# Sums of row quarters formed one stage ahead on GpSimd and stored, left operands built product by product, and a new memory layout, in the feed-forward of a fp32 decoder layer

## The chip, the cores and the metric

The kernel runs on one core of a Trainium2 chip. The metric is the device time of one execution in microseconds (us), the median of several runs. Below, TensorE is PE, VectorE is DVE, ScalarE is ACT, GpSimd is POOL and SyncE, whose queue issues most transfers, is SP.

## The reference

One decoder layer in fp32, sequence 2048, width 1024, feed-forward width 2816. Two groups of attention heads read one normalised input; their normalised outputs go through one output projection. What matters here comes behind that:

```python
x1 = x + concat(groups) @ w_out          # out projection and residual
h  = rmsnorm(x1, g_ffn)
a  = silu(h @ w_gate) * (h @ w_up)       # 1024 -> 2816, twice
y  = rmsnorm(x1 + a @ w_down, g_final)   # 2816 -> 1024
```

## The kernel before, in words

**Precision.** Every fp32 product is three fp32r matmuls: both operands are split into a rounded part (hi) and the rest (lo), and hi·hi, lo·hi and hi·lo are added in PSUM. The split is a cast on ACT and a subtraction on DVE or POOL.

**project_out** works through four blocks t of 512 rows: `add(t, g)` projects one head group and adds the residual on DVE (L903), `norm2(t)` (L905 to L923) squares the rows on ACT, forms their reciprocal root (`rstd_of`, L116 on DVE, L118 on POOL), multiplies them by it (L915, DVE), stores x1 (L911, SP), transposes on PE into PSUM tiles `pt` (L920), copies to `hst` (L921, ACT) and stores the transposed rows into the DRAM scratch `hT` (L923, SP). The order of calls is `add(t, 0)`, `add(t, 1)`, `norm2(t - 1)`.

**ffn_in** computes gate and up for two halves t2 of 1024 rows. A half's left matrix is cut in four quarters (rows by depth), the weights of a column pair j (0 to 10) likewise, and seven products in place of eight make a pair's quad: the left operands are A11, A12, A22 and the sums S1 = A21 + A22, S2 = S1 - A11, S3 = A11 - A21, S4 = A12 - S2; the right ones are T1 to T4 and quarters of the weights. Each product is 12 matmuls of 128x512.

- `operands(t2)` (L960 to L992) makes the 14 left tiles (seven names, hi and lo, 128x4x512). For each k of four it loads two raw buffers `hraw` from `hT` (L969; 512 KB each), forms S1, S2, S3, S4 (L979, L981, L985, L990), casts (L974) and subtracts (L975) pieces of 128x512. In the first half S3 and A12's subtraction are on POOL, A22's always.
- `weights` (L1000 to L1024) loads two raw buffers `wraw_g` or `wraw_u` (L1005, SP), forms T1 (L1011), T2 (L1013), T3 (L1017), T4 (L1021) on DVE and splits all seven (cast L996, subtraction L998).
- `quads` (L1034 to L1060) runs the seven products into three PSUM banks X, Y, Z, where later products are added onto earlier ones; between them c1 is copied on ACT (L1040) and DVE reads u2 (L1043), u3 (L1047), c22 (L1049), c21 (L1055), c12 (L1059). `first_quads` (L1062 to L1087, matmul L1069) is used for the gate of j = 0 of each half: it gives each product a bank and goes by k, so that the matmuls of a k can run when its pieces are there; seven evictions on DVE.
- `fold_down(j)` (L1089 to L1102), in the first half, loads two raw buffers of w_down, sums them on DVE and stores them as `wT`.
- `gated` is silu on ACT; `upped` multiplies (L1125) and sums (L1131 to L1138) on POOL and stores the activations `actS` (L1118) by SP, the last pair's by POOL.

**ffn_out** multiplies the stored activations by w_down with seven products as well: raw `r` (14 buffers), cast L1177, subtraction L1178 into `o` (8 buffers), matmul L1225.

**What sets the order.** The Tile framework schedules the instructions of each engine from the program order and a simulated timeline. Each engine and each queue then runs in order: what stands behind a waiting instruction waits too. One pool of four raw buffers (`rw`, 512 KB each) is shared by project_out's weights, `hraw`, `wraw_g`, `wraw_u` and `draw`; a buffer is given out in turn, and its load waits until its last readers are done. Pools lie one after another in memory, and a tile waits for those that lay at its place.

## Time and profile before

| | us |
|---|---|
| runs of the kernel before | 2407.07, 2409.79, 2407.72 |
| their median | 2407.72 |
| the profiled execution | 2404.51 |
| its span, first to last instruction | 2402.7 |
| project_out's last products, norm2 | until about 1098 |
| gate and up, first half | 1099.5 to about 1540 |
| gate and up, second half | about 1540 to 1976 |
| down projection | from 1976.9 |

The mean granted clock of TensorE is 0.985. The profile is that of one execution. In its views, a row of the windows gives the busy time of each engine in a stretch; a row of the waits gives engine, tile and line that waited, what ended the wait, and the sum, count and longest; a row of a timeline gives start, duration, engine, line, operation, output<-input, shapes, and in brackets the idle time before it and what ended that.

### The profile page before, as it was taken

The page shows a single profiled execution, that of the slowest core. Times are in us where ns is not written, and L with a number is a line of the kernel's source. Part 1 is how long each engine was busy: PE and PEld are TensorE (multiplying, and loading weights), DVE is VectorE, ACT ScalarE, POOL GpSimd, SP SyncE. Part 2 cuts the span into 40 slices and gives each one's busy share as a digit, 9 for nine tenths or more (in the row PEclk, how much of TensorE's full clock was granted, in tenths as well). Part 3 has the DMA queues.
Part 4 walks back from the last instruction along what each step waited for, and adds up shares of the span by engine and source line. Part 5 has one row for each costly group of instructions (what it writes and reads, how often), then busy time and mean ns, then how long its engine had stood idle before and what let it go on. Part 6 is the DMA issues. An engine that isn't in the chain of part 4 may idle for free.

```text
span 2402.7 us, 33903 instructions
## 1 busy us (share of the span) xinstructions
PE 2300.4 (96%) x11765; PEld 1947.0 (81%) x11765; DVE 1604.5 (67%) x3151; ACT 1054.1 (44%) x2371; POOL 468.1 (19%) x418
## 2 busy tenths in 40 slices
PE   7999999997999889897999999899999999999998
PEld 7987788886999878785888888678888878888887
DVE  5335655447999977668877776786666746557555
ACT  5323355453898862336332323342332324444442
POOL 2211211111111010113232232423232330000000
PEclk9999999998999999998999999999999999999999
DMA  7666566659988687755544544333232339768651
GB/s 220 202 189 215 159 188 173 165 157 239 222 222 219 174 244 199 241 171 203 196 155 148 175 149 167 127 127 110 91 120 92 106 115 399 240 198 283 205 189 71
DMA packets 284156, 436.21 MB, mean 182 GB/s; under 512 B 24448, under 2 KB 153088, under 8 KB 278480
## 3 DMA queue, kind: packets, MB, share of 16 engines
q1 hardware_dynamic: 279968, 423.41, 57.5%
q0 software_dynamic: 3728, 10.30, 1.5%
q8 instruction: 93, 1.52, 0.3%
q14 instruction: 79, 0.65, 0.1%
q10 hardware_dynamic: 288, 0.33, 0.0%
HBM read 286.50 MB, written 147.46 MB: 181 GB/s over the span
## 4 chain that ended last, share of the span: by engine, by line
PE 51%; DVE 5%; DMA 4%; issue 1%; POOL 0%; ACT 0%; SPq 0%; DVEq 0%; POOLq 0%; ACTq 0%
PE bY L1225 7%; PE Yu L1031 7%; PE Yg L1031 6%; PE bZ L1225 5%; PE bX L1225 5%; PE Xu L1031 4%; PE Zu L1031 4%; PE Zg L1031 4%; PE Xg L1031 4%; PE acco L893 3%; DMA ob<-oB 1%; DVE wl L998 1%; DMA draw<-in_w_down_dram 1%; DVE xs L915 1%; DMA hraw<-hT 0%
## 5 line engine op out<-in xcount | busy, mean ns | idle before, releaser
L1178 DVE TENSOR_TENSOR o<-r,o 128x1024 fp32r<-128x1024 f32 x154 | 191.2, 1252 | 131.9 <-ACT o L1177 124.1
L1177 ACT CAST o<-r 128x1024 fp32r<-128x1024 f32 x154 | 162.2, 1054 | 225.0 <-DMA r<-in_w_down_dram 50.8
L996 ACT CAST wh<-T 128x512 fp32r<-128x512 f32 x176 | 107.2, 621 | 250.1 <-PE Yu L1031 80.5
L1125 POOL TENSOR_TENSOR c<-c,c 128x512 f32<-128x512 f32 x66 | 105.2, 1594 | 567.9 <-DVE c L1049 389.4
L476 DVE TENSOR_TENSOR hl<-pt,hl 128x512 fp32r<-128x512 f32 (+1 forms) x224 | 145.6, 657 | 81.9 <-ACT hl L475 81.4
L451 ACT ACTIVATE p<-t,m 128x256 f32<-128x256 f32 (+1 forms) x384 | 177.4, 480 | 18.0 <-DVE m L676 18.0
L1225 PE MATMUL bY<-o 128*128 128x512 f32 x792 | 180.5, 389 | 0.0
L1225 PEld LDWEIGHTS bY<-o 128*128 128x128 f32 x792 | 148.6, 188 | 30.9
L177 PE MATMUL acc<-hh,wh 128*128 128x512 f32 x416 | 170.0, 409 | 0.7 <-DVE vt L247 0.7
L177 PE MATMUL acc<-hh,wl 128*128 128x512 f32 x416 | 170.4, 410 | 0.0
L177 PE MATMUL acc<-hl,wh 128*128 128x512 f32 x416 | 169.9, 408 | 0.0
L893 PE MATMUL acco<-woh,oT 128*128 128x512 f32 x512 | 163.4, 397 | 3.7 <-ACT oT L864 3.4
L998 DVE TENSOR_TENSOR wl<-T,wh 128x512 fp32r<-128x512 f32 x176 | 153.2, 882 | 0.3
L494 PE MATMUL o<-hl,v 128*128 128x128 f32 (+1 forms) x816 | 141.8, 294 | 7.2 <-DVE hl L476 5.8
L475 ACT CAST hl<-pt 128x512 fp32r<-128x512 f32 (+1 forms) x224 | 125.3, 569 | 45.2 <-PE pt L470 44.9
L429 PE MATMUL s<-k,q 128*128 128x256 f32 (+1 forms) x768 | 122.1, 290 | 18.7 <-DMA k<-kB 8.8
L470 PE MATMUL pt<-ident,p 128*128 128x128 f32 x848 | 133.7, 279 | 4.8 <-DVE hl L476 2.4
L429 PEld LDWEIGHTS s<-k,q 128*128 128x128 f32 x768 | 100.6, 191 | 26.8 <-DVE nma L566 7.4
L1225 PE MATMUL bX<-o 128*128 128x512 f32 x528 | 120.6, 389 | 1.1 <-DVE o L1178 1.1
L494 PEld LDWEIGHTS o<-hl,v 128*128 128x128 f32 x816 | 111.5, 193 | 12.4 <-DVE hl L476 9.6
L1225 PE MATMUL bZ<-o 128*128 128x512 f32 x528 | 120.3, 389 | 0.0
L893 PEld LDWEIGHTS acco<-woh,oT 128*128 128x128 f32 x512 | 96.8, 189 | 25.4 <-ACT oT L864 4.1
(465 smaller groups left out, 5801.3 us busy)
## 6 DMA issues: line engine op xcount, KB each, us to landing
r<-actS SPq DMA_DIRECT2D x154, 256.0 KB
actS<-c SPq DMA_DIRECT2D x128, 256.0 KB
wraw_g<-in_w_gate_dram SPq DMA_DIRECT2D x44, 512.0 KB
wraw_u<-in_w_up_dram SPq DMA_DIRECT2D x44, 512.0 KB
r<-wT SPq DMA_DIRECT2D x88, 256.0 KB
r<-in_w_down_dram SPq DMA_DIRECT2D x66, 256.0 KB
k<-kB SPq DMA_DIRECT2D x32, 512.0 KB
draw<-in_w_down_dram SPq DMA_DIRECT2D x22, 512.0 KB
```

The lines of the kernel that those rows point to most:

```text
L177: nc.tensor.matmul(acc, a[:, k, :], mv, start=(n == 0), stop=(n == 3 * KC - 1))
L429: nc.tensor.matmul(s[:, i, :n], b["q"], b["k"][m], start=(m == 0), stop=(m == 1))
L451: nc.scalar.activation(b["pv"](p[:, i, :n]), b["tv"](b["t"]), AF.Exp, scale=-1.0, bias=nm[:, c:c + 1], accum_out=l[:, c:c + 1])
L470: nc.tensor.transpose(pt[:, sl, :], p[:, i, hfn * P:(hfn + 1) * P], ident)
L476: nc.vector.tensor_sub(lo, pt[:, a:z, :], hi.bitcast(F32))
L494: nc.tensor.matmul(out, v[:, vi, :], mov, start=(first and n == 1), stop=(last and n == 2 * len(jobs)))
L893: nc.tensor.matmul(acc, oT[kk // 2][:, kk % 2, a, i * P:(i + 1) * P], b[:, kk, :], start=(n == 0), stop=(n == 11))
L998: nc.vector.tensor_sub(lo, src, hi.bitcast(F32))
L1031: nc.tensor.matmul(bank, a[:, k], b[:, k], start=(first and m == 0), stop=(m == 11), skip_group_check=not first)
L1177: nc.scalar.copy(o[:, 0], r)
L1178: V.tensor_sub(o[:, 1], r, o[:, 0].bitcast(F32))
L1225: nc.tensor.matmul(bank[i], o[:, u, 0, i * P:(i + 1) * P], o[:, v, 1, :], start=(first and j == 0 and m == 0), stop=(j == NP - 1 and m == ...
```

## The change

A new DRAM scratch `hS` holds, for each half, the four sums S3, S1, S2, S4. `sum_rows(t2, k)` forms them for one k, in the raw buffers: two SP loads, four POOL instructions on 128x512, two stores of 512 KB through POOL's own queue. For the first half the four calls stand in project_out behind `norm2(1)`; for the second half they stand in the first half of ffn_in, behind the up quad of j = 2, 4, 6 and 8.

`operands` then only loads and splits: for each of the seven names in turn two raw buffers of two k each, 14 loads of 512 KB, 14 casts and 14 subtractions of 128x1024 (12 on DVE, A22's 2 on POOL). `first_quads` is removed; the first gate quad goes through `quads`. The pools are laid in another order with a pad, the left operands in three pools, and in ffn_out `r` has 16 buffers and `o` two pools of four, by j's parity.

```diff
+    sc.hS = pool.tile([NT // 2, 4, P, 4, 512], F32, name="hS")
...
             norm2(t - 1, xs[t - 1])
+            if t == 2:
+                for k in range(4):
+                    sum_rows(nc, rw, sc, 0, k)
         norm2(NT - 1, xs[NT - 1])
+
+
+def sum_rows(nc, rw, sc, t2, k):
+
+    G = nc.gpsimd
+    r, q = (rw.tile([P, 2, 512], F32, tag="raw", name="sraw") for _ in range(2))
+    for a, t in enumerate((r, q)):
+        nc.sync.dma_start(t, sc.hT[2 * t2 + a].rearrange("p (b k) n -> p k b n", b=2)[:, k])
+    G.tensor_add(q[:, 1], q[:, 0], q[:, 1])
+    G.tensor_sub(q[:, 0], r[:, 0], q[:, 0])
+    G.tensor_sub(r[:, 0], q[:, 1], r[:, 0])
+    G.tensor_sub(r[:, 1], r[:, 1], r[:, 0])
+    G.dma_start(sc.hS[t2, 0:2, :, k].rearrange("s p n -> p s n"), q)
+    G.dma_start(sc.hS[t2, 2:4, :, k].rearrange("s p n -> p s n"), r)
...
-        tp, ap, gp, vp, whl, up = (pool(n, b) for n, b in (
-            ("t3", 6), ("a3", 1), ("g3", 6), ("v3", 3), ("whl3", 9), ("u3", 5)))
+        whl, tp, ap0, up, ap2, gp, vp, pad, ap1 = (pool(n, b) for n, b in (
+            ("whl3", 9), ("t3", 6), ("a30", 1), ("u3", 5), ("a32", 1), ("g3", 6), ("v3", 3), ("pad3", 1), ("a31", 1)))
+        pad.tile([P, 80], F32, name="pad3")
+        home = {"A11": ap0, "S2": ap0, "S1": ap1, "S3": ap1, "A12": ap1, "A22": ap2, "S4": ap2}
...
-            e = nc.vector if t2 else nc.gpsimd
-            for k in range(4):
...
+            for n, src in (("A11", sc.hT[2 * t2, :, 0:4]), ("S2", sc.hS[t2, 2]), ("S1", sc.hS[t2, 1]), ("S3", sc.hS[t2, 0]),
+                           ("A12", sc.hT[2 * t2, :, 4:8]), ("A22", sc.hT[2 * t2 + 1, :, 4:8]), ("S4", sc.hS[t2, 3])):
+                for ks in (slice(0, 2), slice(2, 4)):
                     raw = rw.tile([P, 2, 512], F32, tag="raw", name="hraw")
+                    nc.sync.dma_start(raw, src[:, ks])
+                    hi, lo = S[n][0][:, ks], S[n][1][:, ks]
+                    nc.scalar.copy(hi, raw)
+                    (nc.gpsimd if n == "A22" else nc.vector).tensor_sub(lo, raw, hi.bitcast(F32))
...
-                if j:
-                    quads(S, views[0], j, "g", "g", gated)
-                else:
-                    first_quads(S, w0, "g", gated)
+                quads(S, views[0], j, "g", "g", gated, None if j else w0)
                 if t2 == 0:
                     fold_down(j)
                 quads(S, views[1], j, "u", "v", upped)
+                if t2 + 1 < NT // 2 and j in (2, 4, 6, 8):
+                    sum_rows(nc, rw, sc, t2 + 1, j // 2 - 1)
...
-        rp, op, xp, cp, sp = (pool(n, b) for n, b in (("r4", 14), ("op4", 8), ("x4", 3), ("c4", 1), ("s4", 2)))
+        rp, op0, xp, cp, sp, pad, op1 = (pool(n, b) for n, b in (
+            ("r4", 16), ("op40", 4), ("x4", 3), ("c4", 1), ("s4", 2), ("pad4", 1), ("op41", 4)))
+        pad.tile([P, 2900], F32, name="pad4")
```

How the instructions move is shown at three places. The lines of the changed kernel differ by a few: its loads of the sums are L956, the sums L957 to L960, their stores L961 and L962, the loads of the operands L989, their subtraction L992, the weights' load L1006, T1 to T4 L1012 to L1022, the split L999, u3 L1048, the reciprocal root L120, the store of hT L925 and that of x1 L913.

First, SP at the end of project_out, where ffn_in begins. `xs` are rows of x with the residual, `hst` transposed rows. Before (the first gate weights stand some 75 rows further up):

```order
L923 DMA hT<-hst 128x2048 x2
L838 DMA xs_11600<-in_x_dram 128x1024 x3
L969 DMA hraw<-hT 128x2x512
L911 DMA x_71<-xs_11600 128x1024 x4
L969 DMA hraw<-hT 128x2x512
L923 DMA hT<-hst 128x2048 x2
L969 DMA hraw<-hT 128x2x512
L923 DMA hT<-hst 128x2048 x2
L969 DMA hraw<-hT 128x2x512 x4
```

And now:

```order
L925 DMA hT<-hst 128x2048 x2
L840 DMA xs_11641<-in_x_dram 128x1024 x3
L956 DMA sraw<-hT 128x2x512 x7
L913 DMA x_71<-xs_11641 128x1024 x2
L1006 DMA wraw_g<-in_w_gate_dram 128x4x256
L913 DMA x_71<-xs_11641 128x1024 x2
L1006 DMA wraw_g<-in_w_gate_dram 128x4x256
L989 DMA hraw<-hT 128x1024
L925 DMA hT<-hst 128x2048 x2
L989 DMA hraw<-hT 128x1024
L989 DMA hraw<-hS 128x1024 x2
```

The loads of the sums stand ahead of the last stores of x1, and the first gate weights have moved down behind them.

Second, POOL in the same stretch; `rs_o` and `rs_f` are the reciprocal roots of the last add and of norm2. Before:

```order
L118 TENSOR_TENSOR rs_o_11825<-ms_o_11823,half 128x4
L118 TENSOR_TENSOR rs_f_0_11908<-ms_f_0_11906,half 128x1
L118 TENSOR_TENSOR rs_f_1_11928<-ms_f_1_11926,half 128x1
L118 TENSOR_TENSOR rs_f_2_11948<-ms_f_2_11946,half 128x1
L118 TENSOR_TENSOR rs_f_3_11968<-ms_f_3_11966,half 128x1
```

And now:

```order
L957 TENSOR_TENSOR sraw<-sraw 128x512
L120 TENSOR_TENSOR rs_o_11866<-ms_o_11864,half 128x4
L120 TENSOR_TENSOR rs_f_0_11949<-ms_f_0_11947,half 128x1
L958 TENSOR_TENSOR sraw<-sraw 128x512
L959 TENSOR_TENSOR sraw<-sraw 128x512
L961 DMA hS<-sraw 128x2x512
L957 TENSOR_TENSOR sraw<-sraw 128x512
L960 TENSOR_TENSOR sraw<-sraw 128x512
L120 TENSOR_TENSOR rs_f_1_11969<-ms_f_1_11967,half 128x1
L958 TENSOR_TENSOR sraw<-sraw 128x512
```

The roots now stand between the sums of the third and the fourth k and their stores.

Third, DVE in the first half around a sum (the end of j = 4), where the gate weights after next are made; `wl` are lo parts of weights, `T` the sums T1 to T4, `u` and `c` evictions. Before:

```order
L1011 TENSOR_TENSOR T_13768<-wraw_g 128x512
L1047 TENSOR_TENSOR u_13393<-Yu,c_13353 128x512
L1125 TENSOR_TENSOR gate<-Xu,gate 128x512
L998 TENSOR_TENSOR wl<-T_13482,wh 128x512
L1049 TENSOR_TENSOR c_13395<-Zu,u_13393 128x512
L998 TENSOR_TENSOR wl<-wraw_g,wh 128x512
L998 TENSOR_TENSOR wl<-wraw_u,wh 128x512
L1013 TENSOR_TENSOR T_13770<-wraw_g,T_13768 128x512
L1055 TENSOR_TENSOR c_13425<-Yu,c_13353 128x512
```

And now:

```order
L1012 TENSOR_TENSOR T_13785<-wraw_g 128x512
L1056 TENSOR_TENSOR c_13432<-Yu,c_13360 128x512
L999 TENSOR_TENSOR wl<-T_13621,wh 128x512
L1060 TENSOR_TENSOR c_13453<-Zu,u_13374 128x512
L999 TENSOR_TENSOR wl<-T_13633,wh 128x512
L999 TENSOR_TENSOR wl<-wraw_u,wh 128x512
L1014 TENSOR_TENSOR T_13787<-wraw_g,T_13785 128x512
L1018 TENSOR_TENSOR T_13797<-wraw_g 128x512
L1022 TENSOR_TENSOR T_13807<-wraw_g,T_13787 128x512
L1048 TENSOR_TENSOR u_13554<-Yg,c_13514 128x512
```

T1 and T2 have moved behind some of the up quad's evictions, and u3 of the next gate quad (`Yg`) stands right behind T2, T3 and T4.

More of the change, by code (lines that the diff above doesn't have):

```diff
@@ L960, in operands @@
         def operands(t2):
[L962 to L991 removed]
+            S = {n: [p_.tile([P, 4, 512], F32R, tag=f"{n}{u}", name=f"{n}{u}") for u in "hl"] for n, p_ in home.items()}
+            for n, src in (("A11", sc.hT[2 * t2, :, 0:4]), ("S2", sc.hS[t2, 2]), ("S1", sc.hS[t2, 1]), ("S3", sc.hS[t2, 0]),
+                           ("A12", sc.hT[2 * t2, :, 4:8]), ("A22", sc.hT[2 * t2 + 1, :, 4:8]), ("S4", sc.hS[t2, 3])):
+                for ks in (slice(0, 2), slice(2, 4)):
+                    raw = rw.tile([P, 2, 512], F32, tag="raw", name="hraw")
+                    nc.sync.dma_start(raw, src[:, ks])
+                    hi, lo = S[n][0][:, ks], S[n][1][:, ks]
+                    nc.scalar.copy(hi, raw)
+                    (nc.gpsimd if n == "A22" else nc.vector).tensor_sub(lo, raw, hi.bitcast(F32))
             return S
@@ L1032, in product, with quads @@
                     m += 1
-        def quads(S, view, j, nm, tag, done):
-            w = weights(view, j, nm)
+        def quads(S, view, j, nm, tag, done, w=None):
+            w = w or weights(view, j, nm)
             X, Y, Z = (ps.tile([P, 512], F32, tag="mm", name=f"{b}{nm}") for b in "XYZ")
@@ L1059, in quads @@
             nc.vector.tensor_add(c12, Z, u2)
-            done(0, 1, c12, False)
-        def first_quads(S, w, tag, done):
-            bank = {n: ps.tile([P, 512], F32, tag="mm", name=f"F{n}") for n in S}
-            for k in range(4):
-                for n in S:
-                    (hi, lo), (wh, wl) = S[n], w[n]
-                    for m, (a, b) in enumerate(((wh, hi), (wl, hi), (wh, lo))):
-                        nc.tensor.matmul(bank[n], a[:, k], b[:, k], start=(k == 0 and m == 0), stop=(k == 3 and m == 2))
-            c1 = tmp("u", "c1")
-            nc.scalar.copy(c1, bank["A11"])
-            u2 = tmp("u", "u2")
-            nc.vector.tensor_add(u2, bank["S2"], c1)
-            c11 = tmp(tag, "c11")
-            nc.vector.tensor_add(c11, bank["A12"], c1)
-            done(0, 0, c11, False)
-            c12 = tmp(tag, "c12")
-            nc.vector.tensor_add(c12, bank["S1"], u2)
-            u3 = tmp("u", "u3")
-            nc.vector.tensor_add(u3, bank["S3"], u2)
-            c22 = tmp(tag, "c22")
-            nc.vector.tensor_add(c22, bank["S1"], u3)
-            done(1, 1, c22, False)
-            c21 = tmp(tag, "c21")
-            nc.vector.tensor_add(c21, bank["A22"], u3)
-            done(1, 0, c21, False)
-            nc.vector.tensor_add(c12, bank["S4"], c12)
             done(0, 1, c12, False)
@@ L1175, in operands @@
                 nc.sync.dma_start(r[:, 1], wdv[:, f, hf * 512:(hf + 1) * 512])
-            o = op.tile([P, 2, 2, 512], F32R, tag="o", name="o4")
+            o = (op1 if j % 2 else op0).tile([P, 2, 2, 512], F32R, tag="o", name="o4")
             nc.scalar.copy(o[:, 0], r)
```

25 lines of the change are left out of this document (removed).

## The prediction, made blind

> **What bounds the kernel now.** I read the page's busy times first, then the windows over the two starts of the gate and up stage, then TensorE's waits there, then the tile of the loads. The page:
>
> ```profile
> span 2402.7 us, 33903 instructions
> PE 2300.4 (96%) x11765; PEld 1947.0 (81%) x11765; DVE 1604.5 (67%) x3151; ACT 1054.1 (44%) x2371; POOL 468.1 (19%) x418
> ```
>
> TensorE is busy for 96%, so time can be won only where it starves. Windows around the places that the change touches follow; the columns are the stretch, its length, busy us (x instructions) of PE, PEld, DVE, ACT and POOL, the granted clock, the DMA share and GB/s.
>
> ```profile
> 1080.00:1100.00 20.00, 14.08 (x88) 12.11 (x87) 15.57 (x23) 14.04 (x28) 4.33 (x6) 0.93 0.59 219
> 1100.00:1120.00 20.00, 15.74 (x42) 11.16 (x42) 17.48 (x18) 12.13 (x23) 13.32 (x9) 0.65 0.57 205
> 1120.00:1140.00 20.00, 16.22 (x61) 12.07 (x61) 20.00 (x27) 9.92 (x17) 5.76 (x4) 0.91 0.51 169
> 1520.00:1540.00 20.00, 20.00 (x90) 16.54 (x89) 13.62 (x20) 8.13 (x14) 3.24 (x3) 1.00 0.23 77
> 1540.00:1560.00 20.00, 13.57 (x47) 9.19 (x45) 15.83 (x18) 6.63 (x11) 11.98 (x8) 0.83 0.50 165
> 1560.00:1580.00 20.00, 17.16 (x64) 11.01 (x64) 20.00 (x30) 11.45 (x21) 2.76 (x2) 1.00 0.43 140
> 1960.00:1980.00 20.00, 18.11 (x78) 14.31 (x78) 8.96 (x10) 4.96 (x6) 9.29 (x8) 1.00 0.54 181
> ```
>
> An undisturbed stretch does 90 matmuls in 20 us, 0.222 us each. The second start (1540 to 1580) does 111 where 180 would fit: 69 x 0.222 = 15.3 us lost. The first (1100 to 1140) does 103 of 180, 17.1 us lost, behind a stretch of transposes. The start of the next stage (1960 to 1980) does 78 of 90: 2.7 us lost. TensorE's waits name who ends them, with sum, count and longest:
>
> ```profile
> PE FS L1069 <- ACT S3h L974: 5.1, 2, 3.0
> PE FS L1069 <- DVE S2l L975: 4.0, 2, 2.8
> PE pt L920 <- DVE xs L915: 15.5, 7, 4.7
> ```
>
> So both starts wait for left operands, and before the first one the transposes wait for norm2. VectorE is full behind it (20.00 of 20 us in two windows). The tile of the raw loads shows what one piece costs (min/median/max ns):
>
> ```profile
> L974 ACT CAST A11h<-hraw x8: 605/620/624, 1098.9 to 1560.0; 128x512 fp32r<-128x512 f32 x8
> L975 DVE TENSOR_TENSOR A11l<-hraw,A11h x8: 679/693/1775, 1099.5 to 1562.7; 128x512 fp32r<-128x512 f32 x8
> L975 POOL TENSOR_TENSOR A22l<-hraw,A22h x8: 1568/1722/1741, 1102.5 to 1562.9; 128x512 fp32r<-128x512 f32 x8
> ```
>
> **The change part by part.** Prices of the new forms stand in the page's groups (busy us, mean ns):
>
> ```profile
> L1178 DVE TENSOR_TENSOR o<-r,o 128x1024 fp32r<-128x1024 f32 x154 | 191.2, 1252 | 131.9 <-ACT o L1177 124.1
> L1177 ACT CAST o<-r 128x1024 fp32r<-128x1024 f32 x154 | 162.2, 1054 | 225.0 <-DMA r<-in_w_down_dram 50.8
> L1125 POOL TENSOR_TENSOR c<-c,c 128x512 f32<-128x512 f32 x66 | 105.2, 1594 | 567.9 <-DVE c L1049 389.4
> ```
>
> *Second start.* Removed from VectorE: 24 subtractions, 16 sums and 2 of 7 evictions. The two windows from 1540 hold 48 instructions in 35.83 us, 0.746 each, so the old 47 are 35.1 us. The new ones are 12 x 1.252 + 5 x 0.746 = 18.8 us. One wait on GpSimd goes as well:
>
> ```profile
> 1548.44 1.73 DVE L985 TENSOR_TENSOR s<-hraw 128x512 f32<-128x512 f32 x1 [1.16 <-POOL c L1133]
> ```
>
> The 16.3 us freed exceed the 15.3 lost. By product, the casts can also run as each product of the last up quad releases its tile, where the old order by k needed all seven tiles at once. I leave 3 us for what stays: 14 loads turn in four buffers, and two GpSimd subtractions of twice the 1.72 us above come before A22. **-12**, between -15.3 (all) and -3 (the turn of the buffers replaces VectorE as the bound).
>
> *First start.* The order changes most here: the gate weights, loaded long ahead before, stand behind four sums, all through the same four raw buffers. The rows of before:
>
> ```profile
> 1049.69 0.56 SPq L969 DMA_DIRECT2D hraw<-hT  x1
> 1071.66 1.39 POOL L118 TENSOR_TENSOR rs_o<-ms_o,half 128x4 f32<-128x4 f32 x1 [21.94 <-DVE ms_f L116]
> 1095.82 1.28 DVE L915 SCALAR_TENSOR_TENSOR xs<-xs,rs_f,gf 128x1024 f32<-128x1024 f32 x1 [0.72 <-POOL rs_f L118]
> 1099.54 0.80 PE L1069 MATMUL FA<-A11h,wh 128*128 128x512 f32 x1 [0.34 <-ACT A11h L974]
> 1134.29 0.39 PE L1031 MATMUL Xu<-A11h,wh 128*128 128x512 f32 x1
> ```
>
> A load can start at 1049.7 and, by the weight load below, lands 3.6 us later. From 1053.3 GpSimd has 16 x 1.594 = 25.5 us of sums and eight issues of 0.56 (4.5 us): not done before 1083.3, and later by the stores' landings. The reciprocal roots of the last add and of norm2 now stand between these instructions in GpSimd's queue (before they found it idle for 21.94 us). A sum there that waits for its load holds the multiply of L915, and the transposes behind it, which already wait 15.5 us for it. I put that at 3 us: loads of the operands turn from 1102, not 1099. A turn of four is 3.6 + 1.05 + 1.25 and an issue of 0.56, about 6.5 us. Three turns take it to 1121.5, the last pieces of S4 are split at 1127.4, the up weights take the buffers then and land at 1131.0; a cast and a subtraction (0.62 + 0.69) and five instructions ahead on VectorE (three sums of w_down and two evictions, 0.69 each) give 1135.8 for the first up matmul, against 1134.3: **+1.5**. The low end, -4, is no delay of norm2 and a shorter first turn. The high end, +12, is two store landings in series and the roots held by 4 us more.
>
> *The four sums inside the first half.* At the end of j = 2, 4, 6 and 8 the two loads take the place of the next gate weights on SP, and the second weight load waits till a sum's store has landed. VectorE's T2 waits for that load, and the eviction u3 stands behind T2, T3 and T4; the matmuls of A22 may not add to bank Y before u3 has read it. Rows of one such place before, and two that show VectorE's pitch of 0.60:
>
> ```profile
> 1270.63 0.37 SPq L1005 DMA_DIRECT2D wraw_g<-in_w_gate_dram  x1
> 1274.24 0.69 DVE L1013 TENSOR_TENSOR T<-wraw_g,T 128x512 f32<-128x512 f32 x1 [3.04 <-DMA wraw_g<-in_w_gate_dram]
> 1265.11 0.69 DVE L1017 TENSOR_TENSOR T<-wraw_u 128x512 f32<-128x512 f32 x1
> 1265.71 0.69 DVE L1021 TENSOR_TENSOR T<-wraw_u,T 128x512 f32<-128x512 f32 x1
> 1282.72 0.39 PE L1031 MATMUL Yg<-S3h,wh 128*128 128x512 f32 x1
> 1285.44 0.39 PE L1031 MATMUL Xu<-A11h,wh 128*128 128x512 f32 x1
> 1290.66 0.39 PE L1031 MATMUL Yg<-A22h,wh 128*128 128x512 f32 x1
> ```
>
> What GpSimd's own stores take to land (the dma view's last number, and the line of the activations' tile, in us):
>
> ```profile
> oA<-rawa POOLq DMA_DIRECT2D x64, 128.0 KB, 3.7
> actS<-c POOLq DMA_DIRECT2D x6, 256.0 KB, 5.8
> DMA to landing us min/median/max: 2.4/5.6/6.5
> L1118 POOL DMA_DIRECT2D actS<-c x6: 539/562/592, 1971.5 to 1985.3; - x6
> ```
>
> No row has 512 KB from GpSimd. I take 4 us, near the 128 KB row: the 256 KB rows fell where the next stage's loads begin. Then: 1270.6 + 3.6 (load) + 4.8 (three GpSimd instructions) + 0.6 (issue) + 4.0 + 3.6 (weights) = 1287.2, and T2, T3, T4, u3 at 0.60 each make 1289.6. In the changed order of j = 5, 7 and 9, A22 comes after the 12 matmuls of Xu and one of Yu, at 1285.44 + 2.72 + 0.23 = 1288.4. So TensorE waits 1.2 us three times and some 0.5 at the first: **+4**, from 0 (landing 2.8 us or less) to +14 (6.5 us).
>
> The Trainium skill (DMA: Bandwidth & Descriptors, Anatomy of one DMA, SWDGE path) gives a GpSimd-issued DMA 2.0 us and its bytes at 436 GB/s. By that, an estimate, 512 KB land in 3.2 us, the stalls would shrink to about 1.5 us in all, and the whole sum would be -10; the trace's 256 KB rows, with a median of 5.6 us, are over twice what the rule makes of them.
>
> *GpSimd beside VectorE.* Those 16 instructions take 25.5 us in which VectorE's own stretch: the row of A11l goes from 0.69 to 1.775 us. This stands in a stretch where VectorE has 6 us free of 20 (13.62 busy), so I cost it at nothing; without that cover it would be up to 25 us x (1 - 0.69/1.775), 15 us.
>
> The Trainium skill (SBUF — State Buffer, Who interferes with whom) says that VectorE and GpSimd share one pair of ports, and that an instruction of VectorE with two SBUF inputs is held by a GpSimd one that reads SBUF. The stretched row agrees with it; it speaks against moving work to GpSimd, but changes no term.
>
> *Start of the last stage.* The new layout and 16 raw buffers let loads start earlier:
>
> ```profile
> 1976.91 13.46 PE L1225 MATMUL bX<-o 128*128 128x512 f32 x58 [1.10 <-DVE o L1178]
> ```
>
> Of 2.7 us lost, this 1.1 can go: **-1** (0 to -2.7); the rest of the stage runs without a wait, so more buffers bring nothing there.
>
> Sum: -12 + 1.5 + 4 - 1 = -7.5. The profiled execution took 2404.5 us (span 2402.7), so 2397.0 there; it lay 3.2 below the median of the runs, 2407.7, on which the forecast stands: **2400.2**.
>
> **Rivals.**
>
> *The hops are cheap.* Stores land within 2.8 us: no stall at the sums, and the first start gains its 4: -12 - 4 - 1 = -17, 2390.7. For it: the 2.4 us minimum above; against it: that row's median of 5.6. The 3.2 us that the Trainium skill gives (same section as above) lie close to it.
>
> *The gain is given back.* With stores that land in 5 to 5.6 us, each of three sums stalls 2.4 and the first 1 (+8), and the first start is 4 late: -12 + 8 + 4 - 1 = -1, 2406.7. For it: the very median; against it: the DMA share is 0.23 to 0.57 in the windows above, not full.
>
> *Slower: the raw buffers are the bound.* Four buffers now carry operands, weights, w_down and sums, and a sum holds two of them for load, arithmetic and store. If a store takes 6.5 us, the stalls come to 14; in the first project_out, GpSimd's roots stand behind sums that wait for these same buffers, +10: -12 + 14 + 10 - 1 = +11, 2418.7. It decides as soon as stalls and first start together exceed 17.8 us. For it: L915 is already waited for, by 15.5 us; against it: the landing would have to be the slowest of those rows every time.
>
> That the change does less than it says (VectorE's work at the second start isn't what bounds it) is the -3 end of the first term: +1.5, within the third case.
>
> **How the numbers follow.** Forecast (-5 to -12): 0.38. Cheap hops: 0.18. Given back: 0.20. Slower: 0.24. A change of 0.2%, 4.8 us, is about what a measurement of this kernel can tell from none. Faster is the first two, 0.56; the same 0.20; slower 0.24. The range goes from 2389 (cheap hops with a little more) to 2419 (the slower case's own time), leaving out the best ends of all terms and the slower case's tail, some 0.17; the forecast's own range is 2395.7 to 2402.7.
>
> **What would show it.** Right: the second start at 170 or more matmuls in its 40 us, waits there of 3 us at most; VectorE behind T2 at the sums of j = 4, 6, 8 with TensorE idle 1 to 1.5 us ahead of A22; stores from GpSimd landing near 4 us; the first up matmul near 1136. Wrong: TensorE waiting for raw loads in the second start; L915 waiting for GpSimd by more than 4 us in all more than now; landings near 6 us; or a wait that is in none of these places, above all of evictions behind stretched VectorE work.

## The result and the profile after

The changed kernel took 2429.47 us (median of 4 runs, 2428.33 to 2431.27), the kernel before 2408.76 beside it: a ratio of 1.0087, 95% interval 1.007 to 1.0105. It is slower by 20.7 us, outside the forecast's range (2389 to 2419) and on the other side.

The page after:

```profile
span 2427.2 us, 33945 instructions
PE 2318.6 (96%) x11765; PEld 1956.7 (81%) x11765; DVE 1592.6 (66%) x3099; ACT 1051.7 (43%) x2343; POOL 504.4 (21%) x454
```

TensorE has the same 11765 matmuls and is busy for 18 us longer; the span grew by 24.5. The windows of the changed kernel, columns as in the prediction:

```profile
1080.00:1100.00 20.00, 14.04 (x76) 11.77 (x74) 17.84 (x25) 11.04 (x20) 18.82 (x18) 0.83 0.85 308
1100.00:1120.00 20.00, 12.05 (x46) 8.53 (x46) 13.40 (x16) 12.27 (x21) 0.56 (x1) 0.83 0.97 370
1120.00:1140.00 20.00, 15.83 (x57) 10.50 (x55) 13.04 (x13) 11.77 (x13) 4.70 (x2) 0.91 0.76 260
1220.00:1240.00 20.00, 16.97 (x67) 13.48 (x67) 16.07 (x22) 5.66 (x10) 2.41 (x3) 0.91 0.62 214
1240.00:1260.00 20.00, 18.65 (x81) 14.77 (x80) 13.85 (x18) 4.87 (x9) 5.42 (x4) 1.00 0.39 131
1560.00:1580.00 20.00, 20.00 (x89) 16.43 (x88) 15.66 (x17) 10.65 (x12) 9.03 (x5) 1.00 0.77 263
1580.00:1600.00 20.00, 17.67 (x70) 13.88 (x69) 20.00 (x25) 9.31 (x17) 8.80 (x5) 0.91 0.66 207
```

The second start (now about 1547 to 1609) lost only one stretch, 70 matmuls where 90 fit. TensorE's waits there sum to 2.3 us, 1.5 for u3 and 0.8 for an up weight; none is for a left operand any more. The middle of the first half now has holes (67 and 81), in stretches that were full before:

```profile
1220.00:1240.00 20.00, 20.00 (x90) 16.57 (x89) 14.85 (x25) 6.91 (x12) 1.62 (x1) 1.00 0.58 195
1240.00:1260.00 20.00, 20.00 (x90) 16.57 (x89) 13.81 (x18) 6.81 (x13) 9.59 (x6) 1.00 0.39 136
```

And a full stretch does 89 matmuls, not 90. Longer windows show that last point better, one in the second half of gate and up and one in the last stage, in both of which TensorE waits for nothing. Before, then after:

```profile
1760.00:1800.00 40.00, 40.00 (x178) 33.12 (x177) 27.40 (x36) 12.87 (x23) 11.40 (x7) 1.00 0.30 100
2280.00:2320.00 40.00, 40.00 (x178) 33.12 (x177) 20.16 (x19) 15.69 (x15) 0.00 (x0) 1.00 0.62 196
```

```profile
1760.00:1800.00 40.00, 40.00 (x177) 32.85 (x176) 25.50 (x35) 12.76 (x22) 12.67 (x8) 1.00 0.32 104
2280.00:2320.00 40.00, 40.00 (x176) 32.78 (x175) 20.68 (x19) 17.28 (x23) 0.00 (x0) 1.00 0.62 196
```

At the same granted clock of 1.00 and with an engine that is busy throughout, fewer matmuls fit. The traces hold each matmul's start. The mean distance between successive starts (those above 300 ns, the stalls, left out) is the pitch used below: 226.7 ns before in both places, 228.5 and 229.3 after.

With the same starts the whole difference can be cut at equal places of the work: the first matmul of the out projection, the first of gate and up, matmuls number 168, 1764 and 2016 of their 3696, their last, and the last of the down projection.

| stretch (us) | before | after | difference | forecast |
|---|---|---|---|---|
| until the out projection | 875.1 | 878.1 | +3.0 | 0 |
| out projection, norm2 | 224.4 | 226.8 | +2.4 | first start: |
| first start, matmuls to 168 | 55.6 | 58.7 | +3.1 | +1.5 for both |
| rest of the first half, to 1764 | 364.9 | 383.8 | +18.9 | +4 |
| second start, to 2016 | 72.8 | 62.0 | -10.8 | -12 |
| rest of the second half | 381.7 | 384.6 | +2.9 | 0 |
| last stage | 420.3 | 425.1 | +4.8 | -1 |
| behind it | 7.9 | 8.2 | +0.3 | 0 |

In the rest of the first half, distances above 260 ns sum to 2.7 us beyond that bound before and to 17.9 after: +15.2 is stall, the rest pitch. Not all of the stall is waiting: 3.6 of the 17.9 us are 28 matmuls started 0.26 to 0.5 us apart, a good half of them in two spells of 3.4 us, from 1228.1 and from 1262.3, for which the trace grants a clock of 0.50. These spells stand shortly behind the two longest waits (3.0 and 3.3 us below); the first shows as the 0.91 of the window at 1220. The kernel before has no such spell in this half. The first row is code that the change didn't touch; over the 17 profiles of this study it lies anywhere between 874.5 and 881.9, and it is not explained further.

TensorE's waits in the first half behind the start, before and then after:

```profile
PE Yu L1031 <- DVE u L1043: 1.0, 2, 0.6
PE Yg L1031 <- DVE u L1043: 0.9, 1, 0.9
```

```profile
PE Yg L1032 <- DVE u L1048: 6.8, 4, 3.0
PE Yg L1032 <- DVE u L1044: 4.9, 3, 3.3
PE Yu L1032 <- DVE u L1044: 1.5, 1, 1.5
```

As forecast, TensorE waits for u3 (L1048), and for u2 (L1044) too, which stand on VectorE behind T1 to T4, which wait for weights. SP's waits name what loads of weights wait for in turn, before and then after:

```profile
SPq L1005 <- DMA wT<-draw: 29.9, 16, 4.5
```

```profile
SPq L1006 <- DMA hS<-sraw: 26.9, 4, 8.9
SPq L1006 <- DMA wT<-draw: 20.1, 11, 3.1
```

Four times a load of weights waited for the store of a sum, 6.7 us on average. Before, the only stores that such loads waited for were those of `fold_down`, 29.9 us in all; now both kinds make 47.0. But VectorE's own waits for gate weights grew by little, from 24.0 to 29.3 us (before, then after):

```profile
DVE T L1013 <- DMA wraw_g<-in_w_gate_dram: 20.3, 10, 3.0
DVE T L1011 <- DMA wraw_g<-in_w_gate_dram: 3.7, 7, 0.8
```

```profile
DVE T L1014 <- DMA wraw_g<-in_w_gate_dram: 16.9, 9, 3.8
DVE T L1012 <- DMA wraw_g<-in_w_gate_dram: 12.4, 8, 3.5
```

So what stands behind such a wait in VectorE's order must count as well as how long it is. The stores themselves (tile hS, ns and then us):

```profile
L961 POOL DMA_DIRECT2D hS<-sraw x8: 733/757/769, 1060.8 to 1454.1; - x8
DMA to landing us min/median/max: 3.2/4.5/5.8
```

### The profile page after: what moved, and what is told of

The parts are those of the page before. It is cut to its first block, busy times and chain, and to the rows that moved or that the text cites. A ratio compares the mean times of both kernels' runs of the same rounds, so it can differ in the third digit from the quotient of the medians.

```text
span 2427.2 us, 33945 instructions
## 1 busy us (share of the span) xinstructions
PE 2318.6 (96%) x11765; PEld 1956.7 (81%) x11765; DVE 1592.6 (66%) x3099; ACT 1051.7 (43%) x2343; POOL 504.4 (21%) x454
## 3 DMA queue, kind: packets, MB, share of 16 engines
q1 hardware_dynamic: 284000, 438.09, 58.6%
## 4 chain that ended last, share of the span: by engine, by line
PE 61%; DMA 14%; DVE 12%; ACT 5%; issue 3%; POOL 3%; SPq 2%; DVEq 0%; POOLq 0%; ACTq 0%
PE bY L1199 7%; PE acc L179 7%; PE Yu L1032 5%; PE bZ L1199 5%; PE bX L1199 5%; PE Yg L1032 5%; PE accv L246 4%; PE s L431 3%; PE Xu L1032 3%; PE Zu L1032 3%; PE Zg L1032 3%; PE Xg L1032 3%; PE pt L472 3%; ACT p L453 2%; DVE wl L999 2%
## 5 line engine op out<-in xcount | busy, mean ns | idle before, releaser
L999 DVE TENSOR_TENSOR wl<-T,wh 128x512 fp32r<-128x512 f32 x176 | 159.7, 915 | 0.2
L496 PEld LDWEIGHTS o<-hl,v 128*128 128x128 f32 x816 | 113.4, 196 | 11.8 <-DVE hl L478 10.4
L435 DVE CUSTOM_DVE_ANT_0 t<-s,tab 128x256 f32<-128x256 f32 (+1 forms) x344 | 113.0, 369 | 9.4 <-PE s L431 6.8
```

What stands on the lines that cost most here:

```text
L496: nc.tensor.matmul(out, v[:, vi, :], mov, start=(first and n == 1), stop=(last and n == 2 * len(jobs)))
L999: nc.vector.tensor_sub(lo, src, hi.bitcast(F32))
```

## The experiments

Two theories stood at the outset. *Placement*: the pitch of a matmul depends on where its two operands lie, and the new layout put them badly. Its rival was traffic: GpSimd and DMA beside the matmuls. *Buffers*: the stalls of the first half come from four raw buffers that now also carry the sums, and from the loads behind them on SP. Its rivals were GpSimd's work beside VectorE and the store through GpSimd's queue.

Each kernel was timed beside the kernel before on the same chip, and the ratios are to that. The sets of runs were on different chips, so between sets the ratios compare better than the medians. The stretches are cut as above, and each row of them is one profiled execution; those of e5 and e10 are the fastest of their kernels' runs, those of e6 and e14 the slowest. From e5 to e14 every kernel also has the pads of e1 and is set against e1's first half (383.6 us).

| run | until out proj. | out proj. | first start | first half | second start | second half | last stage | median, ratio [95%] |
|---|---|---|---|---|---|---|---|---|
| e1_phase | 876.9 | 226.9 | 59.9 | 383.6 | 63.4 | 381.4 | 420.3 | 2424.3, 1.0080 [1.0060, 1.0101] |
| e2_before_shift | 875.3 | 223.0 | 56.1 | 372.6 | 74.0 | 392.8 | 421.1 | 2425.0, 1.0082 [1.0064, 1.0101] |
| e3_first_old | 881.3 | 221.6 | 56.8 | 386.3 | 63.9 | 384.5 | 425.1 | 2428.5, 1.0092 [1.0077, 1.0107] |
| e4_no_math | 879.4 | 226.4 | 59.8 | 390.2 | 62.3 | 384.5 | 425.1 | 2437.1, 1.0131 [1.0114, 1.0147] |
| e5_fold_later | 875.6 | 225.7 | 60.4 | 373.2 | 62.0 | 381.5 | 420.3 | 2414.3, 1.0033 [1.0018, 1.0048] |
| e6_later_first_old | 881.9 | 223.7 | 56.9 | 372.7 | 62.5 | 382.6 | 420.3 | 2404.1, 0.9990 [0.9974, 1.0006] |
| e7_sums_dve | 880.7 | 226.7 | 58.6 | 373.6 | 61.8 | 381.4 | 420.3 | 2413.4, 1.0028 [1.0016, 1.0041] |
| e8_sum_for_fold | 875.7 | 226.3 | 59.0 | 373.7 | 62.2 | 381.4 | 420.3 | 2408.5, 1.0010 [0.9996, 1.0023] |
| e9_later_dve | 876.8 | 225.7 | 60.5 | 370.6 | 64.5 | 381.5 | 420.3 | 2410.0, 1.0005 [0.9994, 1.0015] |
| e10_all | 874.7 | 221.1 | 56.7 | 383.5 | 62.1 | 383.5 | 420.3 | 2416.2, 1.0037 [1.0023, 1.0051] |
| e11_folds_second | 876.1 | 219.8 | 54.5 | 378.1 | 66.6 | 386.2 | 420.3 | 2412.2, 1.0015 [1.0004, 1.0026] |
| e12_sp_store | 876.7 | 221.7 | 56.6 | 370.2 | 62.1 | 384.8 | 420.3 | 2402.8, 0.9986 [0.9968, 1.0005] |
| e13_gpsimd_store | 878.4 | 223.3 | 56.5 | 370.6 | 62.5 | 381.9 | 420.3 | 2402.4, 0.9988 [0.9975, 1.0001] |
| e14_sp_store_folds | 877.8 | 223.4 | 57.0 | 385.1 | 64.2 | 381.7 | 420.3 | 2412.2, 1.0020 [1.0009, 1.0032] |
| e15_before_phase | 874.5 | 222.0 | 56.1 | 367.2 | 72.6 | 381.9 | 420.3 | 2403.9, 1.0001 [0.9987, 1.0014] |

### Placement

The pools' sizes give every tile's address. In the kernel before, both operands of every gate, up and down matmul start at byte 224 modulo 512. The pad of 80 floats (320 bytes) in the changed kernel puts S1, S3 and A12 at 32, and the pad of 2900 puts the operands of every odd j of the last stage at 192. The first run repairs just that.

**e1_phase**

```diff
-        pad.tile([P, 80], F32, name="pad3")
+        pad.tile([P, 128], F32, name="pad3")
...
-        pad.tile([P, 2900], F32, name="pad4")
+        pad.tile([P, 2908], F32, name="pad4")
```

> Only the two pads of the changed kernel are other sizes (80 to 128 and 2900 to 2908 elements), so that all operands of the feed-forward matmuls start at the same byte modulo 512. Theory of placement: the pitch of undisturbed matmuls falls from 229 ns to the 227 ns of the kernel before, 3,700 x 2.3 + 1,850 x 2.6 ns = 13 us less, 2416 us. Rival (the pitch is slower because of GpSimd's and the DMAs' traffic, or by chance of the run): 2429 us as now.

**e2_before_shift** does the opposite to the kernel before: the split weights lie 320 bytes further, all else in place.

```diff
-        tp, ap, gp, vp, whl, up = (pool(n, b) for n, b in (
-            ("t3", 6), ("a3", 1), ("g3", 6), ("v3", 3), ("whl3", 9), ("u3", 5)))
+        tp, ap, gp, vp, pad, whl, up = (pool(n, b) for n, b in (
+            ("t3", 6), ("a3", 1), ("g3", 6), ("v3", 3), ("pad3", 1), ("whl3", 9), ("u3", 5)))
+        pad.tile([P, 80], F32, name="pad3")
```

> The kernel before with a pad of 320 bytes ahead of the split weights in the gate and up stage, nothing else. Theory of placement: its matmuls there go from 227 to about 229 to 230 ns, 3,700 x 2.5 ns = 9 us more, 2418 us, and the last stage stays at 227 ns. Rival (traffic): no change, 2409 us.

The same two windows, of e1_phase first and then of e2_before_shift:

```profile
1760.00:1800.00 40.00, 40.00 (x178) 33.11 (x177) 25.86 (x35) 12.64 (x22) 12.65 (x8) 1.00 0.32 107
2280.00:2320.00 40.00, 40.00 (x178) 33.15 (x177) 20.68 (x19) 17.79 (x23) 0.00 (x0) 1.00 0.62 197
```

```profile
1760.00:1800.00 40.00, 40.00 (x173) 32.25 (x172) 26.11 (x34) 11.99 (x21) 11.58 (x8) 1.00 0.30 99
2280.00:2320.00 40.00, 40.00 (x178) 33.13 (x177) 20.68 (x19) 17.69 (x23) 0.00 (x0) 1.00 0.61 197
```

With one phase in the whole feed-forward the changed kernel is back at 178 in both, with all its sums and DMAs in place; the kernel before falls to 173 in the stage that was shifted (pitch 233.3 ns) and keeps 178 in the other. Placement is shown, and traffic is out. The changed kernel's own second half says the same product by product: S1, S3 and A12, the shifted ones, ran at 228.9 to 230.6 ns from start to start, A11 and A22, which follow shifted ones or stand between them on TensorE, at 229.7 and 228.2, and S2 and S4 at 226.7; in e1 all seven are at 226.7 or 226.8. The size was missed both ways: the shift cost twice what was expected (2425.0 for 2418), and the repair brought 8.0 us in the two undisturbed stretches (384.6 to 381.4 and 425.1 to 420.3), but nothing in the first half (383.6), whose stalls rose from 17.9 to 20.3 us. That VectorE and the loads, not the matmuls, set the pace there is a reading that fits, not a test. Between the two sets of runs the median fell by 5 us, not 13, and the kernel before's own by 2.4; the ratio went only from 1.0087 to 1.0080, which these runs don't tell from no change. What the repair is worth rests on the two stretches.

**e15_before_phase** asks whether the rule holds where the change never was. In the out projection of both kernels the operands differ by 320 bytes.

```diff
-        op, wp0, wp1, cp, sp, xp, hp, slot = (pool(n, b) for n, b in (
-            ("op", 2), ("wo30", 1), ("wo31", 1), ("c3", 1), ("s3", 2), ("x3", 2), ("hst", 2), ("slot", 6)))
+        op, wp0, wp1, cp, sp, xp, hp, pad, slot = (pool(n, b) for n, b in (
+            ("op", 2), ("wo30", 1), ("wo31", 1), ("c3", 1), ("s3", 2), ("x3", 2), ("hst", 2), ("pad5", 1), ("slot", 6)))
+        pad.tile([P, 80], F32, name="pad5")
```

> The kernel before with one edit: the pad of 320 bytes in the out projection. Theory of placement: the pitch of its matmuls falls from 229.2 to 227.4 ns and the out projection gets 1.5 to 2 us shorter; the whole 2 us, too little to be told from none by the times alone. Rival: no change in pitch.

The pitch fell from 229.2 to 227.6 ns and the stretch from 224.4 to 222.0 us. The whole (1.0001) can't be told from none, as expected: the first half was 2 us longer in that profile.

### The first start

**e3_first_old** leaves out the four sums in the out projection and takes `operands(0)` and the first gate quad from the kernel before.

```diff
-            if t == 2:
-                for k in range(4):
-                    sum_rows(nc, rw, sc, 0, k)
...
-                quads(S, views[0], j, "g", "g", gated, None if j else w0)
+                if t2 == 0 and j == 0:
+                    first_quads(S, w0, "g", gated)
+                else:
+                    quads(S, views[0], j, "g", "g", gated, None if j else w0)
```

> The changed kernel with the first half's operands and first gate quad as before (no sums in the out projection); the sums for the second half stay. Theory that the first start lost by its four sums standing ahead of the gate weights and of norm2: the stretch from the first out-projection matmul to the 168th gate and up matmul shortens by about 5 us, 2424 us. Rival (that stretch is only late by chance, or by the placement): at most 1 us less.

Out projection and first start together took 278.4 us, against 285.5 with the sums and 280.0 before: the sums there cost 7.1. The median moved only by 1 us, and the ratio not at all for the better (1.0092 for 1.0087), since the first half behind it was 2.5 and the second start 1.9 us longer, and the untouched part before it 3.2. A part of what the sums cost stands in GpSimd's timeline of the changed kernel:

```profile
1077.07 1.29 POOL L957 TENSOR_TENSOR sraw<-sraw 128x512 f32<-128x512 f32 x1 [6.66 <-DMA sraw<-hT]
1078.32 1.04 POOL L120 TENSOR_TENSOR rs_o<-ms_o,half 128x4 f32<-128x4 f32 x1
```

The third sum waited 6.66 us for a load that had waited for the first sum's store, and the reciprocal root behind it came 6.7 us later than before (1078.32 for 1071.66). From 1040 to 1160 TensorE's transposes waited 7.4 us, for 5.6 before, and its first products 11.6 us for operands and weights, for 8.4. SP took 24.49 us to issue the seven loads of sums in a row:

```profile
1051.47 24.49 SPq L956 DMA_DIRECT2D sraw<-hT  x7
```

### The stalls of the first half

**e4_no_math** leaves out the 16 GpSimd instructions of the sums in the first half (`if t2 == 0:` ahead of them), so that its second half works on rows that were never summed. It keeps the pads of the changed kernel.

> The changed kernel in which the four sums of the first half load and store their raw rows but leave out the four GpSimd instructions each (the second half's S operands are not sums). Theory that GpSimd's trains of instructions keep VectorE waiting: the stalls of TensorE in the first half fall from 18 us to about 6, 2418 us. Rival (the two raw buffers held until the stores have landed, and the gate weights behind them on SP): at most 4 us less, since only 5 of some 16 us of holding go.

It became slower, 390.2 us in the first half with 24.2 us of stalls. The sums' arithmetic is not the cause by itself. Their two raw buffers do hold up loads: at one of the sums SP's timeline and VectorE's wait read

```profile
1277.70 8.87 SPq L956 DMA_DIRECT2D sraw<-hT  x2
1287.78 7.44 SPq L1007 DMA_DIRECT2D wraw_g<-in_w_gate_dram  x2
```

```profile
1293.57 0.69 DVE L1013 TENSOR_TENSOR T<-wraw_g 128x512 f32<-128x512 f32 x1 [7.05 <-DMA wraw_g<-in_w_gate_dram]
```

The second load of the sum got a buffer only 8 us after the first, the gate weights came behind both, and VectorE stood 7.05 us, with evictions behind it. Why it lost more than with the arithmetic is not settled; the order of the engines is another one in that kernel.

**e5_fold_later**: `fold_down`, too, takes two raw buffers for load, sums and store, in each pair of the first half, though its results are needed only in the last stage.

```diff
-                if t2 == 0:
+                if (t2 == 0) == (j not in (2, 4, 6, 8)):
                     fold_down(j)
```

> The changed kernel with operands at one phase (the pads of the run before), and the sums of w_down (fold_down) of j = 2, 4, 6 and 8 moved into the second half, where nothing needs them before the last stage. So each sum of rows takes the two raw buffers that a sum of w_down took. Theory that the four raw buffers and the loads queued behind them on SP cause the stalls: the first half (matmul 168 to 1764) falls from 383.6 us to about 367, its stalls from 20 to 4 us, the second half stays below 384; 2408 us in all. Rival (the sum's own hops or GpSimd's work beside VectorE): the first half stays above 378 us, 2420 us.

The first half fell from 383.6 to 373.2 us, 10.4 of the 16.6 that were expected, its stalls from 20.3 to 10.4, and the second half took the four folds at no cost (381.5). The gate weights came no sooner for it: VectorE waited for them 29.6 us, for 27.9 in e1. What fell is its wait for the raw rows of `fold_down`, from 22.1 to 13.9. So a fold costs not only by its buffers. Its four sums stand in VectorE's queue too, as three rows ahead of the longest stall of the changed kernel show (others stand between them):

```profile
1253.09 0.69 DVE L1014 TENSOR_TENSOR T<-wraw_g,T 128x512 f32<-128x512 f32 x1 [3.77 <-DMA wraw_g<-in_w_gate_dram]
1254.98 1.70 DVE L1070 TENSOR_TENSOR draw<-draw 128x512 f32<-128x512 f32 x1
1261.17 0.68 DVE L1044 TENSOR_TENSOR u<-Yg,c 128x512 f32<-128x512 f32 x1
```

No run gave the sums buffers of their own with all folds in place, so buffers, loads and VectorE's share of a fold are not parted. About half of what is left in e5 is regular: stalls of 1.1 to 1.4 us ahead of A22 in the gate quads of j = 2, 4, 6 and 8. VectorE and GpSimd at one of them:

```profile
1292.19 0.87 DVE L1014 TENSOR_TENSOR T<-wraw_g,T 128x512 f32<-128x512 f32 x1 [0.83 <-DMA wraw_g<-in_w_gate_dram]
1292.99 1.77 DVE L1018 TENSOR_TENSOR T<-wraw_g 128x512 f32<-128x512 f32 x1
1294.68 1.78 DVE L1022 TENSOR_TENSOR T<-wraw_g,T 128x512 f32<-128x512 f32 x1
1296.39 0.68 DVE L1048 TENSOR_TENSOR u<-Yg,c 128x512 f32<-128x512 f32 x1
```

```profile
1292.60 1.62 POOL L1106 TENSOR_TENSOR c<-c,gate 128x512 f32<-128x512 f32 x1
1294.18 1.74 POOL L1108 TENSOR_TENSOR c<-gate,c 128x512 f32<-128x512 f32 x1
```

This is the stall that the prediction described, T2, T3, T4 and u3 behind the late weights, and nearly its size. T3 and T4 took 1.77 and 1.78 us where 0.60 was counted, while GpSimd ran beside them.

**e6_later_first_old** joins this with e3's edit.

> As the run with fold_down moved, and the first half's operands and first gate quad as in the kernel before (no sums in the out projection). Theory: another 6 us at the first start (from the out projection's first matmul to the 168th of gate and up, 279 us instead of 286), 2401 us, faster than both kernels. Rival (what is saved at the start is lost behind it, as in the run with the old first half alone): 2407 us.

Out projection and first start took 280.6 us, the first half 372.7: the saving at the start stayed this time, and the kernel was level with the kernel before (0.9990, interval 0.9974 to 1.0006), 3 us short of the expectation.

**e7_sums_dve** moves the arithmetic of the second half's sums to VectorE, with all folds in place; the stores stay on GpSimd's queue.

```diff
-    G = nc.gpsimd
+    G = nc.vector if t2 else nc.gpsimd
```

> The kernel with one phase in which the arithmetic of the four sums in the first half is on VectorE (16 instructions of 0.69 us) instead of GpSimd, all else the same. Theory of the raw buffers: a sum's buffers come free 3 us earlier, the stalls of the first half fall by 2 to 5 us of 20, 2421 us. Rival (GpSimd's instructions lock VectorE out): they fall by 10 us or more, 2414 us.

By its numbers the rival won: the first half fell by 10 us, to 373.6. Buffers come free sooner as well when four instructions take 0.69 us each, so this run alone can't tell the two.

**e8_sum_for_fold** calls the sums ahead of the up quad, where the moved folds had stood.

> As the run with fold_down moved, but the sums of rows stand in the program where fold_down stood, ahead of the up quad instead of behind it. Theory of the raw buffers and SP's order: the stalls are as small as there or smaller, since SP then has the same order as before the change with other loads in two places: first half 366 us, 2407 us. Rival (the store through GpSimd's queue, behind its work for the up quad, holds the buffers): first half above 372 us.

373.7 us for the first half, like e5: the place within the pair made no difference there (the medians, 2408.5 and 2414.3, lie further apart than these two profiles). The number asked of the theory (366) was missed, and the rival's bound (372) passed.

**e9_later_dve** joins e5 and e7.

> Both remedies of the stalls in the first half at once, with operands at one phase: fold_down of j = 2, 4, 6, 8 moved into the second half, and the sums' arithmetic in the first half on VectorE. If the two work on different parts of the stalls (buffers taken from the rotation; GpSimd's instructions), they add up: 20 us less twice 10, the first half near 366 us. If both shorten the same wait (the gate weights behind a buffer that a sum holds), the first half stays near 371 us.

370.6 us: two remedies of 10 us each make 13 together, not 20. They mostly shorten one wait.

**e10_all** (e6, e7 and the pad of the out projection) and **e11_folds_second** (the same, `fold_down` only `if t2 == 1`).

> As that, with the first half's operands as in the kernel before, and a pad of 320 bytes in the out projection that brings its operands to one phase too. Theory of placement: the pitch of the out projection's matmuls falls from 229.2 to 227 ns, 768 x 2.3 = 2 us, though the change never touched that stage. Whole: first start 6 us better than the changed kernel's, first half 366, second start 62, so some 8 us below the kernel before, 2398 us. Rival: the first half stays at 371 us as the two remedies shorten the same wait, 2403 us.

> As the last, with all eleven sums of w_down in the second half. Theory of the raw buffers: the first half has two fewer buffers to turn in every pair of columns but the four with sums, and falls below the kernel before's 364.9 us, to 363, with its stalls gone; the second half, which had 1 us of stalls, gains no more than 2 us. 2396 us. Rival: the second half, whose loads then queue behind the folds, loses 4 us or more.

Both fell short. In e10 the first half went back to 383.5 us, with stalls of 4.0 to 4.1 at the sums of j = 4, 6 and 8. On VectorE the sum now waits itself for its load, with everything behind it, and one of two subtractions further on is held by GpSimd for 4.55 us (the last section tells of that):

```profile
1271.08 0.69 DVE L955 TENSOR_TENSOR sraw<-sraw 128x512 f32<-128x512 f32 x1 [4.70 <-DMA sraw<-hT]
1277.83 6.25 DVE L1027 TENSOR_TENSOR wl<-T,wh 128x512 fp32r<-128x512 f32 x2
```

The two are not parted. The same edit that gained 10 us in e7 thus cost 13 here (383.5 for the 370.6 of e13, which differs by it alone): the gain is no property of the engine that adds; it hung on that kernel's order. In e11, with no fold left in the first half, it still took 378.1 us, with 15.1 of stalls, so buffers that the folds free do not by themselves end the stalls. The second half lost 4.5 us, as the rival said (4 or more), where the theory allowed 2. The out projection's pitch, 227.5 and 227.4 ns, came as expected.

**e12_sp_store** and its control **e13_gpsimd_store**: e6 with the pad of the out projection; in e12 SP issues the sums' stores.

```diff
-    G.dma_start(sc.hS[t2, 0:2, :, k].rearrange("s p n -> p s n"), q)
-    G.dma_start(sc.hS[t2, 2:4, :, k].rearrange("s p n -> p s n"), r)
+    nc.sync.dma_start(sc.hS[t2, 0:2, :, k].rearrange("s p n -> p s n"), q)
+    nc.sync.dma_start(sc.hS[t2, 2:4, :, k].rearrange("s p n -> p s n"), r)
```

> Operands at one phase (the out projection's too), the first half's operands as in the kernel before, four folds of w_down moved into the second half, the sums of rows on GpSimd as in the changed kernel, but their stores issued by SP. Theory that a store through GpSimd's own queue costs: the issue of 0.75 us stands in GpSimd's train and the landing is longer; the next gate weights wait for it. Then the first half falls from 373 us (the same kernel with GpSimd's stores) to 369 or less; about 2398 us. Rival (SP, in order, waits for the sum and holds the activations' stores and the gate weights behind it): first half 373 us or more.

> The same with the stores through GpSimd's queue, as in the changed kernel. It differs from the run with four folds moved and the first half as before only by the out projection's phase: out projection at 227.4 instead of 229.1 ns, 1 to 2 us less than that run's 2404 us beside 2406 of the kernel before, so faster than the kernel before by 4 us.

370.2 and 370.6 us for the first half: the queue of the store makes no difference there. Both stand 2.7 to 3 us below the kernel before by their medians (2402.8 and 2402.4 beside 2405.45), with intervals that reach 1.0005 and 1.0001: the best versions of the study, and not told from the kernel before.

**e14_sp_store_folds** puts the folds back into e12.

> As the run with the sums' stores issued by SP (first half 370.2 us), but with all sums of w_down back in the first half, as in the changed kernel. Theory of the raw buffers: with two more buffers to turn in four pairs, stalls of 15 to 20 us return, first half 378 to 384 us, 2413 us. Rival (the store through GpSimd's queue was the cause): first half stays at 370 us, 2403 us.

385.1 us, 15 more than e12, by this one edit; by the medians it is 9 more (2412.2 for 2402.8), and e14's profile is that of its slowest run. VectorE's waits for gate weights rose from 33.8 to 42.7 us, those for the raw rows of the folds from 9.9 to 20.1. Sums and folds in the same pairs carry most of the stalls, by the raw buffers and by what the folds add to SP and VectorE together; the store's queue carries none that can be seen.

## Why the prediction was wrong, point by point

**Second start.** Forecast -12, measured -10.8: right in size, and the waits for left operands are gone as forecast. The start was less full than its sign asked, 158 matmuls in the 40 us from 1547 and not 170. Which share VectorE's fewer, larger instructions have in it and which the order by product was not tried.

**The four sums in the first half: the step that failed.** It read "TensorE waits 1.2 us three times and some 0.5 at the first: +4", from 0 to +14. Measured: +15.2 of stalls. The single stall was described well (e5: 1.1 to 1.4 us four times, though in the gate quads of j = 2, 4, 6 and 8, not in those that the prediction names), and the landing of 4 us was near the 4.5 measured. The step failed in counting one delayed gate load at each sum and nothing else. In the changed kernel the pairs of j = 2, 4, 6 and 8 have 7.5 us of stalls, those of j = 1, 3, 5 and 9 another 7.1. Three things stand in its place. A sum's two raw buffers, beside the two of a fold, hold up the loads behind them, by the stalls' places those of the next pair too, and VectorE's sums of w_down stand in the same queue as what waits for these loads: taking the folds out of the sums' pairs brought 10 us (e5), putting them back cost 15 (e14 against e12; 9 by the medians). One of the two longest waits, 3.0 us, came from VectorE being held by GpSimd for 9.06 us. And behind each of the two longest waits TensorE's granted clock was 0.50 for 3.4 us. How the 15.2 divide among buffers, VectorE's queue and its order stays open. The rival "the raw buffers are the bound" had nearly the price, 14, but tied it to stores that take 6.5 us to land; they took 4.5, so that its price agrees in part by luck.

**GpSimd beside VectorE.** "I cost it at nothing" was wrong: VectorE has the time on average, but not behind a late load. In e5 the stretched T3 and T4 stand right ahead of the u3 that TensorE waits for. The Trainium skill (SBUF — State Buffer, Who interferes with whom) says that a VectorE instruction with two SBUF inputs contends with a GpSimd one that reads SBUF, and that the port pair which they share is an exclusive lock. The trace agrees in kind, and the last section shows a case that went further.

**First start.** Forecast +1.5, measured +5.5 (2.4 and 3.1), within the range given. The roots behind the sums on GpSimd were named, at 3 us; the third sum's wait was 6.66.

**The last stage and the layout: the term that was missing.** Forecast -1; measured +4.8, while the wait for `o` that was to go stayed at 1.1 us. The new layout was taken as a matter of when loads may start. It set the phase of the matmuls' operands, and cost 8.0 us in the two stretches where TensorE is the bound (e1). Neither the sum nor a rival held it.

Taken together, of the 24.5 us between the two profiles: 8 us of the layout, 15 of stalls, 5.5 of the first start and 3 of the untouched part of this profile stand against 10.8 gained, which is +21; the rest is the pitch in the first half. That this +21 is near the +20.7 of the medians is chance.

## What to carry to other kernels

A buffer pool that is shared is a resource with a turn time: price a new user by what its hold does to every load behind it for a whole turn, and by what stands behind those loads on the engine that reads them, not by the one load that it displaces; and look for users that need not be there at all (four of the eleven folds could go elsewhere at no cost, all eleven could not). Whenever pools are laid out anew, compare the operands' start addresses of the matmuls modulo 512 bytes before and after, and count matmuls in a window in which TensorE never waits: a pitch that moves there can be placement, as here. A gain in one stretch is kept only if nothing behind it is already at its limit, so a change is summed stretch by stretch, by the work done and not by the clock.

## What the runs showed of the hardware

**The phase of two operands.** Matmuls of 128x512 fp32r follow each other in 226.7 ns when moving operand and weights start at the same byte modulo 512; with the weights 320 bytes further on, modulo 512, gate and up ran at 233.3 (e2); with the moving operand 320 further on the out projection ran at 229.2 (227.3 to 227.6 once padded). In the last stage of the changed kernel both operands of a product always agreed, but the phase changed by 32 bytes from one product to the next: the eight or so matmuls around such a change took 224 to 236 ns from start to start, then 227 again, and where two products in a row came from the same pool there was none of it. Other offsets, and the reason, were not tried, and a period of 128 or 256 bytes would fit these offsets as well as 512.

**VectorE shut out by a train.** One of the two longest waits in the changed kernel's first half, 3.0 us for u3 at 1226.65, had another cause than late weights. VectorE, then GpSimd:

```profile
1213.33 9.66 DVE L999 TENSOR_TENSOR wl<-T,wh 128x512 fp32r<-128x512 f32 x2
1222.91 0.68 DVE L999 TENSOR_TENSOR wl<-wraw_u,wh 128x512 fp32r<-128x512 f32 x1
```

```profile
1214.10 1.31 POOL L1104 TENSOR_TENSOR c<-c,c 128x512 f32<-128x512 f32 x1
1215.35 1.31 POOL L960 TENSOR_TENSOR sraw<-sraw 128x512 f32<-128x512 f32 x1
1216.61 1.30 POOL L1098 TENSOR_TENSOR c<-c,c 128x512 f32<-128x512 f32 x1
1217.86 1.28 POOL L1106 TENSOR_TENSOR c<-c,gate 128x512 f32<-128x512 f32 x1
1219.11 1.28 POOL L1108 TENSOR_TENSOR c<-gate,c 128x512 f32<-128x512 f32 x1
1220.34 0.76 POOL L962 DMA_DIRECT2D hS<-sraw  x1
1221.12 1.31 POOL L1111 TENSOR_TENSOR c<-c,c 128x512 f32<-128x512 f32 x1
```

Of VectorE's two subtractions the second spans 9.06 us (0.68 alone) and ends 0.6 us after GpSimd's queue has run dry at 1222.43. GpSimd ran at 1.3 us each throughout; where the two alternate, each takes 1.7 to 1.8. So a subtraction can be held not for one GpSimd instruction but for all that follow without a gap. It was no single case: at the sums of j = 4, 6 and 8 the changed kernel shows shorter ones of 2.77 us, e1 one of 6.01 us ahead of its stall at j = 4, and e10 three of 4.55 us, each ahead of one of its long stalls. What decides between alternating and holding was not tried.

**GpSimd's stores.** 512 KB landed in 3.2 to 5.8 us, median 4.5. The Trainium skill (DMA: Bandwidth & Descriptors, Anatomy of one DMA, SWDGE path) gives 2.0 us and the bytes at 436 GB/s, which makes, an estimate, 3.2 for that size; that was the best case here.
